# A hybrid encoder trunk: scores in pairs, one product for the meta tokens' values, and output blocks added to the residual in DRAM

## The chip, the core and the metric

The kernel runs on one core of a Trainium2 chip. The metric is the device time of one execution in microseconds (us), lower is better. The engines are named as in the profile: PE (TensorE matmul) with PEld (its weight load), DVE (VectorE), ACT (ScalarE), POOL (GpSimd) and SP (SyncE, which here only issues DMAs). A DMA that adds to its destination (an accumulating DMA) is issued from POOL in this kernel, a plain one from SP.

## What is computed

One inference step of two layers over 656 tokens: 16 meta tokens, 512 prompt tokens and 8 streams of 16 new tokens each. Model width 1024, stored transposed as 8 blocks of 128 channels x 656 tokens. Cut to what matters here:

```python
def trunk_layer(x, p, ...):
    h = rmsnorm(x, p['g_mix'])
    proj = h @ p['w_in']                       # 24 blocks of 128 columns
    # A) attention, 4 heads, two score maps per head: p0 - lam * p1
    oa = diff_attention(qa, k_all, v_all, ...)
    # B) a causal convolution module (ob), C) a gated linear recurrence (oc)
    mix = concatenate([oa, ob, oc])
    x = x + mix @ p['w_out']                   # output projection, residual
    h2 = rmsnorm(x, p['g_ffn'])
    gate, val = split(h2 @ p['w_up'])
    x = x + (gelu(conv3(gate)) * val) @ p['w_down']

def diff_attention(q, k, v, ...):
    s = einsum('bqhcd,bkhcd->bhcqk', q, k) * scale + bias   # c = 0, 1
    p = softmax(where(mask, s, NEG))
    a = p[:, :, 0] - lam * p[:, :, 1]
    return einsum('bhqk,bkhd->bqhd', a, v)
```

## The kernel before

**Products.** A large product runs as three passes with float32r operands (`mm3`, line 398): the weight's high part times the input's high and low parts, and the weight's low part times the input's high part. ACT casts the high part of a weight (`whi`, line 384), DVE subtracts to get the low part (`wlo`, line 385; `ghi`, `glo` where the parts are kept apart). The raw weights come through four buffers (`raw`), so that a weight load can be issued only when the split of an earlier load is done.

**Stages of a layer.** (1) The input projection, 24 column blocks `d_i`, with attention, convolution and recurrence advancing between them as generators. (2) The output projection. Its first six rows of blocks (convolution, recurrence, heads 0 and 1) are the products `d_oa`, for the 8 output blocks m = 0 to 7; the remaining two (heads 2 and 3) are the products `d_ob`, again for m = 0 to 7, with 12 matmuls for each m. (3) The first three column blocks of `w_up` as one group (`e_u`), which take the inputs `hi_h` and `lo_h` made from the finished blocks x(0) to x(7); the norm factor `r_h` of these blocks, which needs all eight; the factors for a Strassen scheme (`factors`, lines 1068 to 1090, on DVE, POOL and ACT); then the feed-forward loop, whose down projections are added into the residual in DRAM.

**The residual.** `xs[m]` is an SBUF tile, `x_scr` (`xdr`) the same eight blocks in DRAM. Before the change every output block m was loaded (`x_in`, line 448, from the kernel's input in layer 0 and from `x_scr` in layer 1) in the `d_oa` loop. `add_x` (line 441, DVE) added the two halves of the `d_oa` product to it from PSUM, and later the two halves of the `d_ob` product; then `x_out` (line 444) wrote the block to `x_scr`, `sq_add` (lines 432, 437) squared and summed it for the norm, and `split` (lines 359, 360) made `hi_h`, `lo_h`.

**Attention.** For each head, queries are in four tiles t = 0 to 3 of 128 rows; tile t sees 144 + 128 t keys. `scores` makes two score maps c = 0, 1 (line 515; the two use different halves of the partitions), which DVE reads from PSUM with bias and maximum (line 517). `turn` transposes the probabilities by 128 keys, counted from key 0, with the last 16 keys left over; `pv` multiplies by the values: tile t takes t + 1 products with 128 keys and one with 16 keys (lines 551, 554, 556), into a PSUM tile `po` of its own.

**What sets the order.** Within a layer's stages (1) to (3) a scheduler orders the instructions of each engine from data dependences, buffers (57 slots of 128 x 656 floats, tag S; 3 + 5 PSUM banks) and the order in which they are written. Each engine then works through its list in that order, SP too: a DMA issue that has to wait holds the issues behind it. Only the feed-forward loop has an order by hand.

Of the kernel before, what the change touches and what calls it, by code (L numbers as in the profile page):

```python
# [13 lines left out]
ALU = mybir.AluOpType  # L14
# [7 lines left out]
T = 656  # L22
# [137 lines left out]
def trunk_kernel(ctx: ExitStack, tc: tile.TileContext, i: dict, o: dict, depth: int = 2):  # L160
# [45 lines left out]
    ident, b64 = sm_("id"), sm_("b64")  # L206
# [235 lines left out]

    def x_out(m):
        nc.sync.dma_start(out=xdr[m], in_=xs[m][:, :T])
# [5 lines left out]
    def tok_major(src, nm):  # L450

        ps = PB(f"tm_{nm}")
        for j in range(4):
            PE.transpose(ps[:, j * 128:(j + 1) * 128], src[:, j * 128:(j + 1) * 128], ident)
        ps2 = PB(f"tm2_{nm}")
        PE.transpose(ps2[:, :128], src[:, 528:656], ident)
        PE.transpose(ps2[:16, 128:256], src[:, 512:528], ident)
        t = S(f"tok_{nm}")
        A.copy(t[:, :512], ps)
        A.copy(t[:, 512:640], ps2[:, :128])  # L460
        t2 = small.tile([16, 128], F32, tag="tok2", name="tok2", bufs=2)
        A.copy(t2, ps2[:16, 128:256])
        return t, t2


    def attention(l, h, got, mix):
# [33 lines left out]
        def scores(t):  # L500
# [7 lines left out]
            ps = PB(f"sc{l}{h}{t}") if t == 0 else None  # L508
            for c in range(2):
                for n in range(nn):  # L510
                    if t > 0:
                        ps, o0 = PB(f"sc{l}{h}{t}{c}{n}"), 0
                    else:
                        o0 = c * 256
                    PE.matmul(ps[:, o0:o0 + w], lhsT=q[64 * c:64 * c + 64, q0:q0 + 128],  # L515
                              rhs=k[64 * c:64 * c + 64, n * w:(n + 1) * w], start=True, stop=True)
                    V.tensor_tensor_reduce(out=p[c][:, n * w:(n + 1) * w], in0=ps[:, o0:o0 + w],
                                           in1=E8[:, TP - nk + n * w:TP - nk + (n + 1) * w], op0=ALU.add, op1=ALU.max,
                                           accum_out=mx[:, n * 2 + c:n * 2 + c + 1], scale=0.125, scalar=-3.0e38)
# [12 lines left out]

        def turn(t):
            nk = 144 + 128 * t
            p = P.pop(t)
            aT = S(f"aT{l}{h}{t}")
            ps = PB(f"aTp{l}{h}{t}")
            for j in range(t + 1):
                PE.transpose(ps[:, j * 128:(j + 1) * 128], p[:, j * 128:(j + 1) * 128], ident)
            ps2 = PB(f"aTq{l}{h}{t}")  # L540
            PE.transpose(ps2[:16, :128], p[:, nk - 16:nk], ident)
            A.copy(aT[:, :(t + 1) * 128], ps[:, :(t + 1) * 128])
            A.copy(aT[:16, 512:640], ps2[:16, :128])
            AT[t] = aT

        def pv(t):
            q0 = 16 + 128 * t
            aT = AT.pop(t)
            po = PB(f"po{l}{h}{t}")
            for j in range(t + 1):  # L550
                PE.matmul(po[:, :128], lhsT=vt[:, j * 128:(j + 1) * 128], rhs=aT[:, j * 128:(j + 1) * 128], start=j == 0,  # L551
                          stop=False)
            if t < 3:
                PE.matmul(po[:, :128], lhsT=vt[:16, (t + 1) * 128:(t + 2) * 128], rhs=aT[:16, 512:640], start=False, stop=True)
            else:
                PE.matmul(po[:, :128], lhsT=vt2, rhs=aT[:16, 512:640], start=False, stop=True)
            A.copy(oh_[:, q0:q0 + 128], po[:, :128])
# [71 lines left out]
        def s_out():  # L629
            a, t = sv["a"], sv["t"]  # L630
            ps = PB(f"sp{l}{h}")
            PE.matmul(ps[:, :128], lhsT=vt[:, 512:640], rhs=a[:, 256:384], start=True, stop=True)
            PE.matmul(ps[:, 128:144], lhsT=vt[:16, 0:128], rhs=a[:16, 384:400], start=True, stop=True)
# [19 lines left out]
        pv(3)  # L653
# [5 lines left out]
        pv(2)  # L659
# [4 lines left out]
        pv(1)  # L664
        s_pv()
        yield
        pv(0)
# [469 lines left out]
    for l in range(depth):  # L1137
# [5 lines left out]
        xsrc = i["x"] if l == 0 else xdr  # L1143
# [24 lines left out]
        with ExitStack() as behind:  # L1168
# [4 lines left out]
            if l == 0:  # L1173
                setup()
        for n in range(3):
            got[order[n]] = evict_r(ps3[n], r, f"e{l}{n}")
# [34 lines left out]
        for m in range(8):  # L1211
            advance(front)
            x_in(m, xsrc)
            ps = gemm(nxt, ka, mix, f"oa{l}{m}", cx)
            add_x(m, ps, cx)
# [10 lines left out]
        for m in range(8):  # L1226
            ps = gemm(nxt, kb, mix, f"ob{l}{m}", cx)
# [81 lines left out]
        def down(n, last=False):  # L1309
# [5 lines left out]
            def step(m):  # L1315
# [8 lines left out]
                def take():  # L1324
                    if not last:

                        d = S(f"dd{l}{n}{m}")
                        for ps, (a, b) in zip(res.pop(m), cy):
                            A.copy(d[:, a:b], ps[:, :b - a])
                        G.dma_start(out=xdr[m][:, a0:T], in_=d[:, a0:T], accum_op=ALU.add)  # L1330
# [159 lines left out]
```

## Time and profile before

| | |
|---|---|
| time, median of 3 runs | 1680.81 us (1680.68 to 1682.55) |
| the profiled execution | 1678.91 us, span of its instructions 1677.1 us |
| PE busy | 1618.5 us, 97% of the span |
| DVE, ACT, POOL busy | 1245.9, 879.1, 566.8 us (74%, 52%, 34%) |
| DMA | 180.56 MB, mean 108 GB/s |
| layer 0: input projection, output projection, from there to the feed-forward loop's steady part | 26 to 310, 310 to 387, 387 to 465 us |
| layer 1: the same | 858 to 1137, 1137 to 1212, 1212 to 1315 us |

Times inside the execution are counted from the span's start. A row of a timeline gives start, duration, engine, line, operation, output and inputs, and in brackets how long the engine had been idle and what ended the wait. A float32 matmul leaves two records, one for each of two passes; a float32r one leaves one. Matmuls are pipelined: one row of `mm3` lasts 0.31 us, but the next starts 0.15 us after it.

### The profile page before, as it was taken

What the parts mean: (1) busy time and instruction counts of PE and PEld (TensorE: products, weight loads), DVE (VectorE), ACT (ScalarE), POOL (GpSimd) and SP (SyncE); (2) the same over time, 40 slices, a digit from 0 to 9 for tenths busy, and PEclk for the clock granted to TensorE, in tenths of its full rate; (3) what the DMA queues carried; (4) which work ended last, traced back from release to release, by engine and by line L of the source; (5) the groups of instructions that cost most, each with busy time, mean ns of one, the idle gap of its engine ahead of it and who ended that gap; (6) DMA issues with size and microseconds to landing.
All of it is one profiled execution on the core that took longest, in us unless ns stands there. A gap on an engine that the chain in (4) does not pass through costs nothing.

```text
span 1677.1 us, 28733 instructions
## 1 busy us (share of the span) xinstructions
PE 1618.5 (97%) x10774; PEld 1527.1 (91%) x10774; DVE 1245.9 (74%) x2391; ACT 879.1 (52%) x1744; POOL 566.8 (34%) x652
## 2 busy tenths in 40 slices
PE   7999999999899999999999999999999999999997
PEld 7898888898899999999998988888988899999997
DVE  6579985769987767666647898856899777777556
ACT  6656576543554444444437556566545444444444
POOL 0102220007556555554001032100276545554420
PEclk9999999999999999999999999999999999999999
DMA  6236441342144444444532364313511344444453
GB/s 226 74 95 160 111 105 36 113 136 99 45 119 102 102 106 106 105 106 112 190 103 81 95 149 98 99 56 130 179 39 51 98 105 102 102 106 99 108 136 122
DMA packets 75003, 180.56 MB, mean 108 GB/s; under 512 B 12752, under 2 KB 18384, under 8 KB 74864
## 3 DMA queue, kind: packets, MB, share of 16 engines
q1 hardware_dynamic: 62192, 149.36, 27.6%
q0 software_dynamic: 12672, 29.37, 11.2%
q8 instruction: 84, 1.38, 0.3%
q14 instruction: 55, 0.45, 0.1%
HBM read 129.80 MB, written 35.46 MB: 99 GB/s over the span
## 4 chain that ended last, share of the span: by engine, by line
PE 78%; DVE 11%; issue 4%; POOL 3%; ACT 2%; DMA 1%; SPq 0%; POOLq 0%; DVEq 0%; ACTq 0%
PE d_dn L398 16%; PE d_i L398 16%; PE d_v L398 12%; PE d_g L398 12%; PE d_oa L398 5%; PE sc L515 2%; PE e_i L398 1%; PE hl L809 1%; PE po L551 1%; DVE fh L1090 1%; DVE wlo L385 1%; PE d_fin L398 1%; PE e_u L398 1%; DVE wlo L992 1%; POOL gv L1299 1%
## 5 line engine op out<-in xcount | busy, mean ns | idle before, releaser
L398 PE MATMUL d_v<-fh,whi 128*128 128x328 f32 (+1 forms) x1120 | 251.8, 312 | 1.6 <-ACT whi L991 1.6
L384 ACT CAST whi<-raw 128x384 fp32r<-128x384 f32 (+2 forms) x243 | 132.6, 548 | 208.8 <-PE d_i L398 76.5
L398 PE MATMUL d_g<-fh,whi 128*128 128x328 f32 (+1 forms) x1008 | 226.5, 312 | 0.3 <-ACT whi L991 0.3
L398 PE MATMUL d_i<-hi_h,whi 128*128 128x328 f32 x672 | 219.3, 326 | 0.0
L398 PE MATMUL d_i<-lo_h,whi 128*128 128x328 f32 x672 | 213.9, 318 | 0.0
L398 PE MATMUL d_i<-hi_h,wlo 128*128 128x328 f32 x672 | 212.9, 317 | 0.0
L398 PE MATMUL d_dn<-hi_g,wlo 128*128 128x328 f32 (+1 forms) x640 | 199.8, 312 | 2.8 <-DVE wlo L385 2.8
L398 PE MATMUL d_dn<-hi_g,whi 128*128 128x328 f32 (+1 forms) x640 | 200.2, 313 | 1.9 <-ACT hi_g L356 1.7
L398 PE MATMUL d_dn<-lo_g,whi 128*128 128x328 f32 (+1 forms) x640 | 200.1, 313 | 1.8 <-DVE lo_g L357 1.8
L385 DVE TENSOR_TENSOR wlo<-raw,whi 128x384 fp32r<-128x384 f32 (+2 forms) x243 | 170.9, 717 | 30.5 <-ACT whi L384 22.7
L398 PEld LDWEIGHTS d_v<-fh,whi 128*128 128x128 f32 x1120 | 189.3, 189 | 2.2 <-ACT whi L991 2.2
L992 DVE TENSOR_TENSOR wlo<-wcb,whi 128x512 fp32r<-128x512 f32 x152 | 131.9, 868 | 74.9 <-ACT whi L991 72.3
L398 PE MATMUL d_v<-fh,wlo 128*128 128x328 f32 (+1 forms) x560 | 175.5, 313 | 3.3 <-DVE wlo L992 3.3
L398 PEld LDWEIGHTS d_g<-fh,whi 128*128 128x128 f32 x1008 | 170.4, 189 | 0.5 <-ACT whi L991 0.5
L398 PE MATMUL d_g<-fh,wlo 128*128 128x328 f32 (+1 forms) x504 | 157.8, 313 | 2.3 <-DVE wlo L992 2.3
L985 POOL TENSOR_TENSOR wcb<-raw 128x512 f32<-128x512 f32 x76 | 109.6, 1442 | 127.8 <-DMA raw<-in_w_up 80.2
L992 DVE TENSOR_TENSOR wlo<-raw,whi 128x512 fp32r<-128x512 f32 x114 | 114.8, 1008 | 50.7 <-ACT whi L991 50.5
L991 ACT CAST whi<-wcb 128x512 fp32r<-128x512 f32 x152 | 93.7, 620 | 110.6 <-PE d_g L398 33.3
L398 PEld LDWEIGHTS d_i<-hi_h,whi 128*128 128x128 f32 x672 | 127.5, 190 | 10.1 <-issue 5.6
L398 PEld LDWEIGHTS d_i<-lo_h,whi 128*128 128x128 f32 x672 | 127.6, 190 | 3.8 <-issue 1.3
L398 PEld LDWEIGHTS d_i<-hi_h,wlo 128*128 128x128 f32 x672 | 127.2, 189 | 3.0 <-issue 1.3
L398 PEld LDWEIGHTS d_dn<-hi_g,wlo 128*128 128x128 f32 x640 | 121.1, 189 | 3.5 <-DVE wlo L385 3.5
(394 smaller groups left out, 4026.9 us busy)
## 6 DMA issues: line engine op xcount, KB each, us to landing
raw<-in_w_up SPq DMA_DIRECT2D x88, 512.0 KB, 3.7
raw<-in_w_in SPq DMA_DIRECT2D x45, 512.0 KB, 3.7
raw<-in_w_down SPq DMA_DIRECT2D x48, 384.0 KB, 3.8
x_scr<-x SPq DMA_DIRECT2D x24, 328.0 KB, 3.2
x_scr<-dd POOLq DMA_DIRECT2D x24, 328.0 KB, 4.5
x<-x_scr SPq DMA_DIRECT2D x24, 328.0 KB, 4.4
x_scr<-dd POOLq DMA_DIRECT2D x24, 320.0 KB, 4.6
cvb<-cvt POOLq DMA_DIRECT2D x20, 328.0 KB, 5.0
```

Of the source, the lines that this page charges most:

```text
L384: seq(A.copy(hi[:, :n], raw[:, a:a + n]))
L385: seq(V.tensor_tensor(out=lo[:, :n], in0=raw[:, a:a + n], in1=hi[:, :n].bitcast(F32), op=ALU.subtract))
L398: PE.matmul(ps[:, :b - a], lhsT=ww[:, n], rhs=r[:, a:b], start=first and j == 0, stop=last and j == 2)
L515: PE.matmul(ps[:, o0:o0 + w], lhsT=q[64 * c:64 * c + 64, q0:q0 + 128], rhs=k[64 * c:64 * c + 64, n * w:(n + 1) * w], start=True, stop=True)
L551: PE.matmul(po[:, :128], lhsT=vt[:, j * 128:(j + 1) * 128], rhs=aT[:, j * 128:(j + 1) * 128], start=j == 0, stop=False)
L809: PE.matmul(ps[:, c * 128:(c + 1) * 128], lhsT=kk[:, 16 + 128 * c:144 + 128 * c], rhs=both(m0 + 64 * c, 64), start=True, stop=True)
L985: G.tensor_tensor(out=t, in0=x, in1=y, op=op)
L991: A.copy(hi, x)
L992: V.tensor_tensor(out=lo, in0=x, in1=hi.bitcast(F32), op=ALU.subtract)
L1090: V.tensor_tensor(out=lo, in0=x, in1=hi.bitcast(F32), op=ALU.subtract)
L1299: G.tensor_tensor(out=v[:, a0:TP], in0=v[:, a0:TP], in1=a[:, a0:TP], op=ALU.mult)
```

## The change

- **Scores.** For each key part the products of c = 0 and c = 1 are issued one after the other, into two PSUM banks, before DVE reads the first of them. For t = 0 both maps shared one bank before.
- **Values.** The blocks of 128 keys now start at key 16 and the 16 meta tokens stand apart. Their probabilities of all four query tiles are kept in one tile `aTm`, and one product of 16 keys x 512 queries (`po`, line 555 of the changed kernel) replaces four of 16 keys x 128. All value products of a head stand in one place, behind its last transposition, in one PSUM bank, and one ACT copy of 512 columns replaces four of 128.
- **First output blocks.** The `d_oa` product goes from PSUM through ACT into a tile `do` (`to_x`), and an accumulating DMA from POOL adds it to `x_scr`. In layer 0 the eight blocks are written to `x_scr` at the start. `x_in(m)` moves from the `d_oa` loop into the `d_ob` loop, where it reads `x_scr`; `add_x`, `x_out`, `sq_add` and `split` of the `d_ob` loop stay.

```diff
+    def to_x(m, ps, cc, nm):
+        d = S(nm)
+        for p, (a, b) in zip(ps, cc):
+            A.copy(d[:, a:b], p[:, :b - a])
+        G.dma_start(out=xdr[m][:, cc[0][0]:T], in_=d[:, cc[0][0]:T], accum_op=ALU.add)
...
-            for c in range(2):
-                for n in range(nn):
-                    if t > 0:
-                        ps, o0 = PB(f"sc{l}{h}{t}{c}{n}"), 0
-                    else:
-                        o0 = c * 256
-                    PE.matmul(ps[:, o0:o0 + w], lhsT=q[64 * c:64 * c + 64, q0:q0 + 128],
+            for n in range(nn):
+                pair = []
+                for c in range(2):
+                    pair.append(PB(f"sc{l}{h}{t}{c}{n}"))
+                    PE.matmul(pair[c][:, :w], lhsT=q[64 * c:64 * c + 64, q0:q0 + 128],
                               rhs=k[64 * c:64 * c + 64, n * w:(n + 1) * w], start=True, stop=True)
-                    V.tensor_tensor_reduce(out=p[c][:, n * w:(n + 1) * w], in0=ps[:, o0:o0 + w],
+                for c in range(2):
+                    V.tensor_tensor_reduce(out=p[c][:, n * w:(n + 1) * w], in0=pair[c][:, :w],
...
+        def pv():
+            po = PB(f"po{l}{h}")
+            PE.matmul(po, lhsT=vt2, rhs=aTm[:16, :512], start=True, stop=False, skip_group_check=True)
+            for t in (3, 2, 1, 0):
+                aT = AT.pop(t)
+                for j in range(t + 1):
+                    PE.matmul(po[:, t * 128:(t + 1) * 128], lhsT=vt[:, j * 128:(j + 1) * 128],
+                              rhs=aT[:, j * 128:(j + 1) * 128], start=False, stop=j == t, skip_group_check=True)
+            A.copy(oh_[:, 16:528], po)
...
             if l == 0:
                 setup()
+                for m in range(8):
+                    x_out(m)
...
         for m in range(8):
             advance(front)
-            x_in(m, xsrc)
             ps = gemm(nxt, ka, mix, f"oa{l}{m}", cx)
-            add_x(m, ps, cx)
+            to_x(m, ps, cx, f"do{l}{m}")
...
         for m in range(8):
+            x_in(m, xdr)
             ps = gemm(nxt, kb, mix, f"ob{l}{m}", cx)
             add_x(m, ps, cx)
             x_out(m)
```

SP's list in layer 0, from the last loads of the `d_oa` loop to the blocks' way out. Before (`x` with its number is the tile of one block):

```order
L448 DMA x_3954<-in_x 128x656
L448 DMA x_4006<-in_x 128x656
L367 DMA raw<-in_w_up 128x1024
L976 DMA gpast_4062<-in_state_ffn 128x352
L367 DMA raw<-in_w_up 128x1024 x2
L367 DMA raw<-in_w_out 128x256 x7
L444 DMA x_scr<-x_3460 128x656
L367 DMA raw<-in_w_up 128x1024
L444 DMA x_scr<-x_3598 128x656
L367 DMA raw<-in_w_up 128x1024
L444 DMA x_scr<-x_3718 128x656
L444 DMA x_scr<-x_3798 128x656
```

And SP's list of the changed kernel at the same place:

```order
L977 DMA gpast_4042<-in_state_ffn 128x352
L367 DMA raw<-in_w_out 128x256 x3
L455 DMA x_4074<-x_scr 128x656
L367 DMA raw<-in_w_out 128x256 x2
L367 DMA raw<-in_w_up 128x1024
L451 DMA x_scr<-x_4074 128x656
L455 DMA x_4105<-x_scr 128x656
L367 DMA raw<-in_w_up 128x1024
L451 DMA x_scr<-x_4105 128x656
L455 DMA x_4137<-x_scr 128x656
L367 DMA raw<-in_w_up 128x1024
L451 DMA x_scr<-x_4137 128x656
```

Before, all eight loads stood ahead of the first write; now the load of block m + 1 stands behind the write of block m, for all eight blocks and in both layers. The first three loads of `w_up` stand ahead of `gpast` in the changed list.

PE's list at the last value product of head 0 in layer 0 (`po` the output, `aT` the transposed probabilities, `tok_v` the values). Before, where the other three tiles' products stand 53 to 192 rows earlier:

```order
L551 MATMUL po_1396<-aT_1275,tok_v_652 128x128
L554 MATMUL po_1396<-aT_1275,tok_v_652 128x128
```

And now:

```order
L555 MATMUL po_1388<-aTm_667,tok_663 128x512
L559 MATMUL po_1388<-aT_866,tok_v_660 128x128 x4
L559 MATMUL po_1388<-aT_985,tok_v_660 128x128 x3
L559 MATMUL po_1388<-aT_1144,tok_v_660 128x128 x2
L559 MATMUL po_1388<-aT_1272,tok_v_660 128x128
```

The ten products with 128 keys moved to one place, and one of 512 columns stands ahead of them in place of four of 128 columns.

## Rows read from the trace of the kernel before

**Rows 1.** The page, parts 1 and 5: busy times; one group of splits.

```profile
PE 1618.5 (97%) x10774; PEld 1527.1 (91%) x10774; DVE 1245.9 (74%) x2391; ACT 879.1 (52%) x1744; POOL 566.8 (34%) x652
...
L385 DVE TENSOR_TENSOR wlo<-raw,whi 128x384 fp32r<-128x384 f32 (+2 forms) x243 | 170.9, 717 | 30.5 <-ACT whi L384 22.7
```

**Rows 2.** Busy time by stretch: length, PE, PEld, DVE, ACT, POOL, clock, DMA.

```profile
257.00:310.00 53.00, 52.23 (x346) 44.89 (x339) 32.56 (x75) 33.47 (x72) 1.69 (x8) 1.00 0.19 60
310.00:369.40 59.40, 58.63 (x416) 54.20 (x417) 36.26 (x92) 30.19 (x74) 2.45 (x5) 1.00 0.38 123
369.40:397.80 28.40, 24.51 (x153) 23.04 (x153) 26.68 (x39) 17.44 (x29) 12.84 (x8) 1.00 0.58 198
397.80:465.00 67.20, 60.31 (x379) 58.00 (x377) 62.10 (x89) 31.46 (x60) 43.91 (x49) 0.97 0.11 33
```

**Rows 3.** Timeline of SP in layer 0's last down projection, where blocks are reloaded.

```profile
821.89 0.40 SPq L448 DMA_DIRECT2D x<-x_scr  x1
...
826.98 0.32 SPq L444 DMA_DIRECT2D x_scr<-x  x1
827.41 0.37 SPq L448 DMA_DIRECT2D x<-x_scr  x1
...
848.66 0.37 SPq L448 DMA_DIRECT2D x<-x_scr  x1
```

**Rows 4.** Timeline of DVE in the same stretch: the additions that wait for these loads.

```profile
830.88 0.91 DVE L441 TENSOR_TENSOR x<-d_dn,x 128x328 f32<-128x328 f32 x2 [0.46 <-DMA x<-x_scr]
...
853.82 0.91 DVE L441 TENSOR_TENSOR x<-d_dn,x 128x328 f32<-128x328 f32 x2 [3.13 <-DMA x<-x_scr]
```

**Rows 5.** Timelines of PE and DVE, layer 0, from `d_ob` to the factors.

```profile
369.24 0.31 PE L398 MATMUL d_ob<-hi_mx,whi 128*128 128x328 f32 x1
...
386.70 0.31 PE L398 MATMUL d_ob<-hi_mx,wlo 128*128 128x328 f32 x1
...
388.49 0.48 DVE L441 TENSOR_TENSOR x<-d_ob,x 128x328 f32<-128x328 f32 x1
...
391.90 0.83 DVE L437 TENSOR_TENSOR sq<-sq,sq 128x656 f32<-128x656 f32 x1
...
396.25 1.48 DVE L319 SCALAR_TENSOR_TENSOR r_h<-rt_h,r_h 128x656 f32<-128x656 f32 x1
397.77 12.38 DVE L1068 SCALAR_TENSOR_TENSOR x<-x,cst,r_h 128x656 f32<-128x656 f32 x8
...
419.60 0.39 PE L398 MATMUL d_g<-hi_h,ghi 128*128 128x328 f32 x1 [0.74 <-DVE gp L1248]
...
422.56 0.64 PE L398 MATMUL d_g<-hi_h,glo 128*128 128x328 f32 x1 [2.41 <-DVE glo L385]
```

**Rows 6.** Timeline of DVE, layer 1: the norm factor's last instruction.

```profile
1221.13 1.23 DVE L319 SCALAR_TENSOR_TENSOR r_h<-rt_h,r_h 128x644 f32<-128x644 f32 x1
```

**Rows 7.** PE at head 0's values, layer 0; a float32 product of 328 columns.

```profile
92.07 1.16 PE L551 MATMUL po<-aT,tok_v 128*128 128x128 f32 x8
93.16 0.48 PE L556 MATMUL po<-aT,tok 16*128 16x128 f32 x2
93.57 0.55 PE L539 MATMUL aTp<-cst,p 128*128 128x128 f32 x3
...
264.36 2.21 PE np_ln L314 x8
```

**Rows 8.** Timeline of PE: one score product of tile 0, and the next.

```profile
107.73 0.51 PE L515 MATMUL sc<-e,e 64*128 64x144 f32 x2
108.17 0.42 PE L611 MATMUL sa<-selw,pown 96*128 96x48 f32 x2
```

**Rows 9.** Short stretches around PE's waits in rows 5, columns as in rows 2.

```profile
420.00:424.00 4.00, 1.59 (x6) 1.45 (x6) 3.86 (x7) 3.78 (x5) 2.56 (x9) 0.80 0.00 0
424.00:428.00 4.00, 4.00 (x23) 4.00 (x22) 3.26 (x6) 3.52 (x7) 3.28 (x2) 0.78 0.41 131
428.00:432.00 4.00, 4.00 (x29) 4.00 (x28) 3.25 (x10) 3.62 (x10) 1.94 (x3) 1.00 0.42 131
```

More of the change, by code (lines that the diff above doesn't have):

```diff
@@ L453, in tok_major @@
         for j in range(4):
-            PE.transpose(ps[:, j * 128:(j + 1) * 128], src[:, j * 128:(j + 1) * 128], ident)
+            PE.transpose(ps[:, j * 128:(j + 1) * 128], src[:, 16 + j * 128:144 + j * 128], ident)
         ps2 = PB(f"tm2_{nm}")
         PE.transpose(ps2[:, :128], src[:, 528:656], ident)
-        PE.transpose(ps2[:16, 128:256], src[:, 512:528], ident)
+        PE.transpose(ps2[:16, 128:256], src[:, 0:16], ident)
         t = S(f"tok_{nm}")
@@ L507, in scores @@
             w = nk // nn
-            ps = PB(f"sc{l}{h}{t}") if t == 0 else None
-            for c in range(2):
-                for n in range(nn):
-                    if t > 0:
-                        ps, o0 = PB(f"sc{l}{h}{t}{c}{n}"), 0
-                    else:
-                        o0 = c * 256
-                    PE.matmul(ps[:, o0:o0 + w], lhsT=q[64 * c:64 * c + 64, q0:q0 + 128],
+            for n in range(nn):
[3 more added lines that the diff above has]
+                    PE.matmul(pair[c][:, :w], lhsT=q[64 * c:64 * c + 64, q0:q0 + 128],
                               rhs=k[64 * c:64 * c + 64, n * w:(n + 1) * w], start=True, stop=True)
-                    V.tensor_tensor_reduce(out=p[c][:, n * w:(n + 1) * w], in0=ps[:, o0:o0 + w],
+                for c in range(2):
+                    V.tensor_tensor_reduce(out=p[c][:, n * w:(n + 1) * w], in0=pair[c][:, :w],
                                            in1=E8[:, TP - nk + n * w:TP - nk + (n + 1) * w], op0=ALU.add, op1=ALU.max,
@@ L531, in scores @@
             P[t] = p[0]
+        aTm = S(f"aTm{l}{h}")
         def turn(t):
-            nk = 144 + 128 * t
             p = P.pop(t)
@@ L538, in turn @@
             for j in range(t + 1):
-                PE.transpose(ps[:, j * 128:(j + 1) * 128], p[:, j * 128:(j + 1) * 128], ident)
+                PE.transpose(ps[:, j * 128:(j + 1) * 128], p[:, 16 + j * 128:144 + j * 128], ident)
             ps2 = PB(f"aTq{l}{h}{t}")
-            PE.transpose(ps2[:16, :128], p[:, nk - 16:nk], ident)
+            PE.transpose(ps2[:16, :128], p[:, 0:16], ident)
             A.copy(aT[:, :(t + 1) * 128], ps[:, :(t + 1) * 128])
-            A.copy(aT[:16, 512:640], ps2[:16, :128])
+            A.copy(aTm[:16, t * 128:(t + 1) * 128], ps2[:16, :128])
             AT[t] = aT
[L546 to L557, printed above, removed]
+        def pv():
[7 more added lines that the diff above has]
+            A.copy(oh_[:, 16:528], po)
         x = qx[h % 2]
@@ L632, in s_out @@
             PE.matmul(ps[:, :128], lhsT=vt[:, 512:640], rhs=a[:, 256:384], start=True, stop=True)
-            PE.matmul(ps[:, 128:144], lhsT=vt[:16, 0:128], rhs=a[:16, 384:400], start=True, stop=True)
+            PE.matmul(ps[:, 128:144], lhsT=vt2, rhs=a[:16, 384:400], start=True, stop=True)
             for g in range(2):
@@ L652, in attention @@
         yield
-        pv(3)
         turn(2)
@@ L658, in attention @@
         turn(1)
-        pv(2)
         s_turn()
@@ L663, in attention @@
         turn(0)
-        pv(1)
         s_pv()
         yield
-        pv(0)
+        pv()
         s_out()
@@ L1142, in trunk_kernel @@
         col = [cols[a] // 128 + b for a, b in order]
-        xsrc = i["x"] if l == 0 else xdr
         got, mix = {}, {}
@@ L1325, in take @@
                     if not last:
[L1327 to L1330, printed above, removed]
+                        to_x(m, res.pop(m), cy, f"dd{l}{n}{m}")
                     else:
```

## The prediction

> **What bounds the kernel now.** I read the page's shares first: PE is busy for 97% of the span [rows 1], so what is taken off another engine is worth nothing unless PE waits for it. Then the busy times by stretch: in the input projection and in the stage of the `d_oa` products PE works 52.23 of 53.0 and 58.63 of 59.4 us, while from `d_ob` to the factors it works 24.51 of 28.4 and DVE 26.68, and in the stretch behind that 60.31 of 67.2 and DVE 62.10 [rows 2]. So there are two kinds of place. In the first two stretches PE is the bound, and a matmul less is time won, one for one. Around `d_ob` DVE is as full as PE, and who waits for whom has to be read from the timelines. There the first `d_ob` matmul starts at 369.24 and the last at 386.70; the last half of block 7 is added at 388.49; the squares are summed at 391.90; the norm factor `r_h` is ready at 397.73 (396.25 + 1.48); the factors follow at once; and PE, done with `e_u` and one further product, twice waits for DVE, 0.74 us for `gp` and 2.41 us for `glo`, both behind the factors on DVE [rows 5]. So in this stage the end is set by DVE's list from `r_h` on, and `r_h` waits for block 7. Call the start of the first `d_ob` matmul S: `r_h` is ready at S + 28.5.
>
> **The change, part by part.**
>
> *Blocks reloaded in the `d_ob` loop.* This is the large term. SP's list now reads, for each block, load, write, next load. SP works through its list in order, so the load of block m + 1 is issued only when the write of block m could be, that is when DVE has finished block m. That finish in turn waits for the load of block m. The eight loads have become a chain of eight, where all were ahead before.
>
> The trace has this very chain. In layer 0's last down projection the blocks are reloaded and written in the same order on SP. There a load follows the write by 0.43 us (826.98 to 827.41) [rows 3]; the addition starts when the load has landed, 3.47 us after the issue (827.41 to 830.88) in one case and 5.16 (848.66 to 853.82) in another, each time with DVE idle until then [rows 3, 4]; and both halves are added in 0.91 us [rows 4]. From 821.89 to 848.66 there are five steps in 26.77 us, 5.35 each [rows 3]. Each step there also holds one 512 KB weight load beside the load and the write of a block, as most of the first steps do here. I take 5.4 us; the bounds are 4.8 (3.47 + 0.91 + 0.43) and 6.5 (5.16 + 0.91 + 0.43).
>
> The chain's start: the load of block 0 stands behind weight loads whose buffers are freed by splits of `w_up` on DVE, and four such splits are now queued behind the low parts of heads 2 and 3 when the `d_oa` products end. At 0.72 us for a split [rows 1] I estimate S + 3.8 for its issue, between S and S + 5.5 (all splits first). With 4.0 us to its landing (5.35 - 0.91 - 0.43) and seven steps of 5.4, the addition of block 7 starts at S + 45.6 and ends 0.9 later, at S + 46.5. Before, 3.8 us passed from its end to the end of the sum of squares (388.97 to 392.73), with splits between them that now lie in the chain's gaps: I take 1.7, the square and the sum at about 0.83 each. From the sum to `r_h` it is 5.0 us (392.73 to 397.73) [rows 5]. So `r_h` is ready at S + 53.2 instead of S + 28.5: 24.7 us later.
>
> Is there cover? PE is ahead by its banks only: three banks hold the `d_ob` products, so PE stops after a block and a half, and the last two thirds of `e_u` need banks that block 7 frees. Those 123 matmuls at 0.15 us, the norm's product (about 1) and one product of 48 matmuls (7.2) then end at about S + 46 + 27 = S + 73. `glo`, for which PE waited at 422.56 (S + 53.3) [rows 5], comes 24.7 later, at S + 78. So DVE still ends last and the whole 24.7 us stand on the path. In layer 1 `r_h` was ready at 1222.36 [rows 6], 27.9 us after its first `d_ob` matmul by the same reading; there I take 25.0. Together **+49.7 us**, bounds +34 (steps of 4.8, first load at S + 1) and +66 (steps of 6.5).
>
> *A page on this price.* The Trainium skill, "DMA: Bandwidth & Descriptors", section "Anatomy of one DMA", fits 2.0 us and bytes / 436e3 (for transfers issued by GpSimd). For a block of 335,872 bytes that is an estimate of 2.8 us where the rows show 3.47 to 5.16; the step would be 4.1 us and the result some 23 us lower than mine. The measured rows decide.
>
> *Output blocks through ACT and POOL.* In the `d_oa` stage 16 additions on DVE for each layer go, 16 copies on ACT and 8 accumulating DMAs on POOL come. DVE worked 36.26, ACT 30.19 and POOL 2.45 of 59.4 us there and PE 58.63 [rows 2]: nothing is won by lighter DVE, and 16 copies of about the same half microsecond bring ACT to some 38, which PE covers. A copy that comes late would hold one of three banks, which gives PE about 2.7 us before it notices (18 matmuls at 0.15). I take 0. The eight writes at the start of layer 0 put 8 x 0.43 = 3.4 us [rows 3] ahead of four weight loads on SP; those weights are needed only after the first three blocks and one more, so I take 0, bounds 0 and 3.4.
>
> *Values.* Four products with 128 keys took 1.09 us (92.07 to 93.16), 0.27 each, and the one with 16 keys 0.41 (93.16 to 93.57) [rows 7]. A head has ten of the first and four of the second: 4.3 us. A product of 512 columns is priced from 328 columns, 2.21 us for 8 passes or 0.276 for a pass [rows 7]: two passes of 512/328 x 0.276 are 0.86 us. A head now costs 2.7 + 0.86 = 3.6, 0.77 us less; eight heads 6.2 us, nearly all where PE is the bound. Putting the products in one place saves further entries into a run of small products; I add 1 us.
>
> *Scores.* For t = 0 a product of 144 columns took 0.44 us (107.73 to 108.17) [rows 8], alone; two side by side on different halves of the partitions may share time. From 0 to 0.44 us for each of 8 heads: I take 1 us. The other tiles had separate banks already. DVE, ACT and POOL keep their work and are covered by PE. Longer lives of the transposed probabilities (four more slots of 57 for each head) may make a tile wait for a slot: bounds 0 and 8 us for all heads. Attention together: **-8 us**, bounds -13 and +2.
>
> **Sum.** 49.7 - 8 = +41.7 on the profiled execution's 1678.91 us: 1720.6. The median of three lies 1.9 above that execution, so the forecast is **1723 us**, 2.5% slower.
>
> **The rivals.**
> - *Not slower: the loads stay ahead.* If an issue that waits did not hold the issues behind it, all loads would have landed before `d_ob`, the chain would vanish and -8 us remain: 1673 us. It decides at a step of about 1.9 us, (28.5 - 0.9 - 1.7 - 5.0 - 7.8) / 7 with the same start. Against it: DVE's idle rows that end with the load, one step after another [rows 4]. 3%.
> - *The clock falls and stays low.* PE will work 1.8 us (12 matmuls) of each 5.4. After PE had waited in 420 to 424 the granted clock was 0.80 there and 0.78 in the next 4 us, and 1.00 after that [rows 9]: between them 3.4 us at the lower of its two levels (1.2 instead of 2.4 GHz), 1.7 us lost. In the `d_ob` loop even doubled matmuls (3.6 us) fit into a step, and 1.7 us in `e_u` fit under the 5 us between S + 73 and S + 78. But if all of `e_u`'s rest ran at the lower level, 18.5 us more less 5 of cover would be added in each layer: +27, 1750 us. 7%. The Trainium skill, "TensorE: Matmul & The Clock Gate", section "HAM oscillation", speaks for it: it says that where PE's work for each block is shorter than the wait for the next block's DMA, PE falls back to the lower clock for every block. The rows here agree that a wait brings the clock down, and show it recovering.
> - *Every load is as slow as the slowest row.* The accumulating DMAs of the last blocks, the writes and 512 KB loads share the queues: 5.16 instead of 4.0 for each is 8 x 1.1 x 2 = +18, 1741 us. 9%.
> - *Slots cost what the products save.* Attention at +2 instead of -8: 1733 us. 7%.
> - *The first load is early and the steps short* (4.8): 1708 us. 9%.
>
> **How the numbers follow.** The forecast has 65%, the rivals 35%. The range for 8 in 10 is **1706 to 1744 us**: below, the shortest step; above, the slowest loads; 1673 and 1750 stay outside. A measurement of this kernel tells apart about 0.2%, 3.4 us. Slower by more than that: all but the first rival and an unnamed rest, **0.95**; within 0.2%: **0.02**; faster: **0.03**.
>
> **What would show it.** In SP's timeline around S: write and load side by side, 0.43 us apart, eight pairs some 5.4 us from each other. On DVE: `x<-d_ob` with idle time that ends with the load of `x`. On PE: waits of `d_ob` and `e_u` for DVE of some 3 us each, 20 to 25 us in each layer, and a lower granted clock there. `r_h` ready about 53 us after the first `d_ob`, and `d_g` still waiting for `glo`. The input projection shorter by about 8 us over both layers. The prediction is wrong if the loads are issued without waiting for the writes, if PE's wait for `glo` vanishes (then `e_u` ends last), or if the input projection is longer than before.

## The result, and the profile after

The changed kernel takes **1729.59 us** (median of 5, 1724.44 to 1733.73) against 1682.18 us for the kernel before, run beside it: a ratio of 1.028, 95% interval 1.0258 to 1.0302. It is 2.8% slower; the forecast was 2.5% and 1723 us, range 1706 to 1744. The profiled execution took 1726.23 us with a span of 1724.5, which is 47.4 us more than the span of before (1677.1).

The first view is part 1 of the page of the changed kernel:

```profile
PE 1632.0 (95%) x10726; PEld 1536.6 (89%) x10726; DVE 1222.5 (71%) x2359; ACT 888.1 (51%) x1752; POOL 582.3 (34%) x668
```

Beside [rows 1], PE has 48 matmul records less and is "busy" 13.5 us longer, yet its share falls: there is new idle time, and some of the work runs at a lower clock. Where the 47.4 us lie is read from the first row of each tile in PE's timelines and the last instruction of `r_h` on DVE:

| stretch (us) | before | after | difference |
|---|---|---|---|
| start to the first `d_i`, layer 0 | 42.4 | 44.4 | +2.0 |
| first `d_i` to first `d_ob`, layer 0 | 326.8 | 325.4 | -1.5 |
| first `d_ob` to `r_h` ready, layer 0 | 28.5 | 54.3 | **+25.8** |
| `r_h` to the first down projection, layer 0 | 63.6 | 61.7 | -1.9 |
| from there to the first `d_i` of layer 1 | 408.7 | 407.6 | -1.0 |
| first `d_i` to first `d_ob`, layer 1 | 324.3 | 325.2 | +0.8 |
| first `d_ob` to `r_h` ready, layer 1 | 28.1 | 52.5 | **+24.4** |
| `r_h` to the first down projection, layer 1 | 90.5 | 88.5 | -2.0 |
| from there to the end | 364.2 | 365.0 | +0.7 |

All of the loss is in the two `d_ob` stages, and the gain that was expected of attention is missing. SP's timeline of the changed kernel in layer 0, where S, the first `d_ob`, is at 369.75:

```profile
374.92 0.44 SPq L455 DMA_DIRECT2D x<-x_scr  x1
...
380.52 0.33 SPq L451 DMA_DIRECT2D x_scr<-x  x1
380.90 0.42 SPq L455 DMA_DIRECT2D x<-x_scr  x1
...
385.81 0.32 SPq L451 DMA_DIRECT2D x_scr<-x  x1
386.23 0.37 SPq L455 DMA_DIRECT2D x<-x_scr  x1
...
412.45 0.32 SPq L451 DMA_DIRECT2D x_scr<-x  x1
412.87 0.37 SPq L455 DMA_DIRECT2D x<-x_scr  x1
```

A load stands 0.37 to 0.43 us behind each write, and from the second load (380.90) to the eighth (412.87) there are six steps, 5.33 us on average (4.58 to 6.65). DVE's timeline in the same stretch:

```profile
384.87 0.91 DVE L441 TENSOR_TENSOR x<-d_ob,x 128x328 f32<-128x328 f32 x2 [1.59 <-DMA x<-x_scr]
387.33 1.60 DVE L360 SCALAR_TENSOR_TENSOR lo_h<-x,cst,hi_h 128x656 fp32r<-128x656 f32 x1 [1.55 <-ACT hi_h L359]
388.85 0.41 DVE L385 TENSOR_TENSOR wlo<-raw,whi 128x256 fp32r<-128x256 f32 x1
389.95 0.91 DVE L441 TENSOR_TENSOR x<-d_ob,x 128x328 f32<-128x328 f32 x2 [0.69 <-DMA x<-x_scr]
...
396.60 0.91 DVE L441 TENSOR_TENSOR x<-d_ob,x 128x328 f32<-128x328 f32 x2 [2.19 <-DMA x<-x_scr]
...
401.25 0.89 DVE L441 TENSOR_TENSOR x<-d_ob,x 128x328 f32<-128x328 f32 x2
...
416.96 0.89 DVE L441 TENSOR_TENSOR x<-d_ob,x 128x328 f32<-128x328 f32 x2
...
423.16 0.84 DVE L319 SCALAR_TENSOR_TENSOR r_h<-rt_h,r_h 128x656 f32<-128x656 f32 x1
```

The additions of five of the eight blocks wait for their loads, as forecast; those of the other three (at 401.25, 405.89 and 416.96) follow DVE's own work without a pause. And most of the 4 us that a load takes is filled by a sequence of DVE's own: 1.55 us of waiting for ACT's `hi_h`, then `lo_h`, then the split of a weight, and only then the next addition. DVE's waits from S to `r_h` (us in total, times, longest), and busy times of that stretch in both kernels (length, PE, PEld, DVE, ACT, POOL, clock, DMA), after first:

```profile
DVE lo_h L360 <- ACT hi_h L359: 10.9, 7, 1.6
DVE x L441 <- DMA x<-x_scr: 6.8, 5, 2.2
DVE wlo L385 <- ACT whi L384: 2.8, 2, 1.7
```

```profile
369.75:424.00 54.25, 35.31 (x158) 32.13 (x157) 30.90 (x45) 21.58 (x37) 15.93 (x11) 0.72 0.56 171
```

```profile
369.24:397.73 28.49, 24.60 (x155) 23.13 (x154) 26.65 (x38) 17.56 (x29) 12.77 (x8) 1.00 0.58 198
```

DVE was busy for 26.65 of 28.49 us before; now it is busy for 30.90 and idle for 23.35. Of the 25.8 us that were added, 4.3 are work and 21.5 idle time, and only 6.8 of the idle time ends with a load. That is the reading which the experiments had to settle. PE's side of it, its waits in that stretch and behind it:

```profile
PE d_ob L398 <- DVE x L441: 18.6, 7, 6.9
...
PE d_g L398 <- DVE glo L385: 1.8, 1, 1.8
```

PE waits 18.6 us for additions and later still 1.8 us for `glo`, where it waited 2.41 before [rows 5]: DVE's list ends last, as before.

### The profile page after: what moved, and what is told of

Same layout as the page of the kernel before. It is cut to its first block, busy times and chain, and to the rows that moved or that the text cites. A ratio compares the mean times of both kernels' runs of the same rounds, so it can differ in the third digit from the quotient of the medians.

```text
span 1724.5 us, 28685 instructions
## 1 busy us (share of the span) xinstructions
PE 1632.0 (95%) x10726; PEld 1536.6 (89%) x10726; DVE 1222.5 (71%) x2359; ACT 888.1 (51%) x1752; POOL 582.3 (34%) x668
## 5 line engine op out<-in xcount | busy, mean ns | idle before, releaser
L385 DVE TENSOR_TENSOR wlo<-raw,whi 128x384 fp32r<-128x384 f32 (+2 forms) x243 | 164.3, 691 | 55.1 <-ACT whi L384 51.4
```

The lines of the kernel that those rows point to most:

```text
L385: seq(V.tensor_tensor(out=lo[:, :n], in0=raw[:, a:a + n], in1=hi[:, :n].bitcast(F32), op=ALU.subtract))
```

## The experiments

All times are medians beside the kernel before on the same chip (1679.75 to 1680.32 us there). The last column is the time from the first `d_ob` to `r_h` in layers 0 and 1; it is 28.5 and 28.1 before and 54.3 and 52.5 in the changed kernel.

| kernel | us | ratio to before, 95% | `d_ob` to `r_h`, us |
|---|---|---|---|
| attn_only | 1680.06 | 0.9991 to 1.0012 | 28.3, 27.9 |
| out_only | 1725.63 | 1.0258 to 1.0289 | 53.5, 53.0 |
| load_1ahead | 1709.70 | 1.0160 to 1.0208 | 45.4, 42.7 |
| loads_ahead | 1703.53 | 1.0129 to 1.0162 | 40.6, 41.2 |
| loads_pool | 1701.14 | 1.0107 to 1.0141 | 37.5, 35.9 |
| writes_pool | 1721.48 | 1.0224 to 1.0266 | 51.0, 49.7 |
| split_lag | 1724.69 | 1.0250 to 1.0286 | 53.4, 51.4 |
| writes_pool_split_lag | 1720.05 | 1.0227 to 1.0258 | 49.6, 49.3 |
| attn_values | 1680.69 | 0.9995 to 1.0012 | 28.2, 28.0 |
| values_in_place | 1673.71 | 0.9946 to 0.9974 | 28.3, 28.1 |
| values_in_place2 | 1673.23 | 0.9945 to 0.9973 | 28.2, 28.1 |
| values_in_place_old_scores | 1676.56 | 0.9970 to 0.9988 | 28.3, 28.0 |

### The two parts alone: attn_only, out_only

attn_only is the changed kernel with the old output blocks (`...` marks what is cut):

```diff
-                for m in range(8):
-                    x_out(m)
...
+            x_in(m, xsrc)
             ps = gemm(nxt, ka, mix, f"oa{l}{m}", cx)
-            to_x(m, ps, cx, f"do{l}{m}")
+            add_x(m, ps, cx)
...
-            x_in(m, xdr)
             ps = gemm(nxt, kb, mix, f"ob{l}{m}", cx)
```

out_only is the kernel before with just these lines as in the changed one.

> The attention part alone (scores in pairs, values in one place with one product for the meta tokens); the output blocks take the old way through add_x, with the loads in the d_oa loop. Theory A (the prediction's price of the products holds, and the output blocks' new way takes part of it back at the start and in the d_oa stage): 8 us less than before, 1674. Theory B (the products save about half of that; the marks in the trace of the changed kernel stand 2.3 us closer from the first d_i to the first d_oa in layer 0 and 1.5 in layer 1): 1678, or 4 us less than before. Theory C (what the products save is lost to later values, longer lives and DVE): within 1.5 us of before.

> The output blocks' part alone (d_oa products through ACT and an accumulating DMA, blocks reloaded in the d_ob loop, eight writes at the start); attention as before. The chain of loads behind writes is in it whole. By the prediction +49.7 us, 1732. Theory A (attention saved 8 in the changed kernel): 1738. Theory B (attention saved 4): 1734. Theory C (attention saved nothing): 1730.

The attention part moves nothing (theory C: 1680.06 against 1680.32), and the output blocks carry the loss: 45 us (1725.63), with the same 53 us from `d_ob` to `r_h`. That is below all three values expected of out_only (1730 to 1738): its two `d_ob` stages are longer by 49.9 us, as priced, but from `r_h` to the first down projection each layer is 2 us shorter. In out_only the stage of the `d_oa` products lasts 59.35 us (59.37 before): the copies on ACT and the accumulating DMAs cost nothing there, as forecast.

### Loads ahead of the writes: loads_ahead, load_1ahead, loads_pool

```diff
             to_x(m, ps, cx, f"do{l}{m}")
+            if m > 1:
+                x_in(m - 2, xdr)
...
+        for m in (6, 7):
+            x_in(m, xdr)
         gpast = ffn_state(l)
...
-            x_in(m, xdr)
             ps = gemm(nxt, kb, mix, f"ob{l}{m}", cx)
```

load_1ahead writes `x_in(0)` ahead of `gpast` and `x_in(m + 1)` in place of `x_in(m)`. loads_pool is loads_ahead with these loads issued from `nc.gpsimd` instead of `nc.sync`.

> The changed kernel with the load of block m written two blocks behind its accumulating DMA in the d_oa loop, so that on SP seven of the eight loads of a layer stand ahead of the first write of a block. Chain theory (each load waits on SP behind the write of the block before): both layers lose the 25 us again, 1680 us, r_h some 29 us behind the first d_ob. Rival (the loads are late because the additions in DRAM land late, or because a load behind an accumulating DMA is slow): the wait moves along with the load, 1715 to 1730 us. Rival (loads that wait on SP now hold the weight loads of the d_oa stage): d_ob starts later than 60 us after the first d_oa, 1690 us or more.

> The changed kernel with each load written one block earlier: on SP load 3 then stands behind write 1, load 5 behind write 3, load 7 behind write 5, and load 1 behind write 0, so that half as many round trips are on the chain. Chain theory: four steps of 5.3 us less in each layer, some 21 less wherever nothing else comes last, so that r_h is some 33 to 38 us behind the first d_ob and the time 1690 to 1700 us. Rival (the price is of the loads themselves and not of their order): within 5 us of the changed kernel, 1725 to 1730 us.

> As loads_ahead, but the loads of the blocks are issued from POOL, two blocks behind the accumulating DMA there, so that SP's list holds no load that waits for an addition in DRAM, and the w_out loads of the d_ob products do not stand behind one. In loads_ahead r_h was still 40.6 us behind the first d_ob (28.5 before), and DVE waited 4.24 us for a weight whose load stood on SP behind the load of block 7. Chain theory with that second cause (SP's order, once for the blocks, once for the weights): r_h about 29 to 33 us behind the first d_ob in both layers and 1680 to 1688 us. Rival (the remaining 12 us are of blocks that land late whatever the queue, or of DVE's extra load): r_h stays near 40 us, 1700 us or more.

The direction is the chain's, the size is not. The changed kernel stood 47.4 us above the kernel before that was run beside it. With loads one block earlier 29.4 us of that are left, so that 18 are won where 30 to 40 were expected; with all loads ahead 23.2 (loads_ahead) and 21.4 (loads_pool) are left, so that 24 to 26 are won, not the 50 of the chain theory. In loads_ahead, SP's list shows a second wait of its own kind:

```profile
368.48 1.46 SPq L455 DMA_DIRECT2D x<-x_scr  x2
...
376.75 0.32 SPq L455 DMA_DIRECT2D x<-x_scr  x1
...
379.56 0.38 SPq L367 DMA_DIRECT2D raw<-in_w_out  x1
```

The eighth load has to wait for its addition in DRAM until 376.75 and holds the weight loads of the later `d_ob` blocks. The first of these goes out at 379.56, ACT casts it at 382.96 after 6.61 us without work, and DVE waits 4.24 us for that, until 383.40. Issued from POOL (loads_pool) the loads hold no weight load, and that stage is 3 to 5 us shorter, but the time is only 2.4 us lower: 1701, where the rival had 1700 or more. What is left there, DVE's waits and busy times in loads_pool from S (371.88) to `r_h`:

```profile
DVE rt_h L317 <- ACT rt_h L316: 2.2, 2, 1.7
DVE wlo L385 <- ACT whi L384: 2.0, 2, 1.1
DVE lo_h L360 <- ACT hi_h L359: 0.9, 1, 0.9
```

```profile
371.88:409.40 37.52, 30.49 (x168) 27.13 (x167) 31.29 (x46) 21.50 (x38) 16.05 (x13) 0.91 0.62 197
```

No wait for a load of a block is left, and the waits for `hi_h` are down from 10.9 to 0.9 us: DVE's list is staggered again, with additions of later blocks ahead of an earlier block's `lo_h`. The stage is still 9.0 us longer than before: 4.6 are DVE's work (31.29 against 26.65) and 4.4 idle time. The work is a move. Six `glo` splits, 4.1 us, stand in this stretch in loads_pool and in the changed kernel (3.9 us there), while in the kernel before DVE did them in the `d_oa` stage:

```profile
L385 DVE TENSOR_TENSOR glo<-raw,ghi 128x512 fp32r<-128x512 f32 x6 | 4.0, 688 | 0.4 <-ACT ghi L384 0.4
```

(groups of DVE by line in the kernel before, 310 to 370 us). These six stand in the `d_ob` stage of both layers in every kernel with the output blocks' edit, out_only too, and in the `d_oa` stage in every kernel without it, so it is that edit that moves them. Which of its lines made the scheduler place them later was not isolated. In layer 1 the stage is 7.8 us longer than before; the two stages make 16.8 of the 21 us that loads_pool still loses.

### Cutting the chain without moving the loads: writes_pool, split_lag, both

```diff
             add_x(m, ps, cx)
-            x_out(m)
+            x_out(m, nc.gpsimd)
```

split_lag leaves the writes on SP and puts `hs.append(split(xs[m - 2], ...))` in the place of block m's, the last two behind the loop; writes_pool_split_lag has both edits.

> The changed kernel with one edit: the write of each block in the d_ob loop is issued from POOL instead of SP. The loads keep their place in the d_ob loop, behind weight loads, but none stands behind a write any more. Chain theory (it is the write on the same queue that holds the next load): the steps of 5.3 us vanish, loads go as the weight buffers allow, r_h 30 to 40 us behind the first d_ob, 1685 to 1705 us. Rival (the loads' late place in the program is what costs, whichever queue the writes take): within 5 us of the changed kernel, 1725 to 1730 us.

> The changed kernel with one edit: in the d_ob loop the split of block m (hi_h on ACT, lo_h on DVE) is written two blocks later, so that DVE's list holds the addition of block m + 1 ahead of lo_h of block m. The writes stay on SP. In writes_pool DVE still went block by block, some 4.7 us each: addition, 1.55 us of waiting for hi_h, lo_h, a split of a weight, next addition. Theory of two chains, one on SP (5.3 us a block), one on DVE's list right under it (4.6 to 4.7): with the SP chain left in place this edit gives nothing, 1726 to 1733 us, DVE's waits for hi_h become waits for the load. Rival (DVE's list alone sets the steps, SP's order follows it): 20 us or more less than the changed kernel, below 1710.

> Both edits: writes of the d_ob loop from POOL, and each split two blocks later. Theory of two chains: with both cut, a load waits only behind a weight load whose buffer a split on DVE frees, for which I estimate some 3.3 us a block instead of 5.3 from the rows of writes_pool; 14 us less in each layer than the changed kernel, 1695 to 1706 us, r_h about 40 us behind the first d_ob. Rival (the loads' late place costs what it costs, whatever is cut): as writes_pool, 1717 us or more.

writes_pool was to decide between the chain and the loads' late place, and it speaks mostly for the place: 1721.48, outside both expectations, is 41.7 us above the kernel before, only some 6 us less than the changed kernel's 47.4 (the intervals overlap slightly), although no load stands behind a write. DVE's waits there, and one of its steps:

```profile
DVE lo_h L360 <- ACT hi_h L359: 10.9, 7, 1.6
...
DVE x L441 <- DMA x<-x_scr: 1.9, 3, 1.4
```

```profile
390.93 0.91 DVE L441 TENSOR_TENSOR x<-d_ob,x 128x328 f32<-128x328 f32 x2 [0.18 <-DMA x<-x_scr]
393.38 1.75 DVE L360 SCALAR_TENSOR_TENSOR lo_h<-x,cst,hi_h 128x656 fp32r<-128x656 f32 x1 [1.55 <-ACT hi_h L359]
395.06 0.68 DVE L385 TENSOR_TENSOR wlo<-raw,whi 128x512 fp32r<-128x512 f32 x1
395.66 0.89 DVE L441 TENSOR_TENSOR x<-d_ob,x 128x328 f32<-128x328 f32 x2
```

The waits for loads fall from 6.8 to 1.9 us and those for `hi_h` stay at 10.9. So there are two chains of nearly the same period. One runs over SP (write, load, addition; 5.33 us on average in the changed kernel). The other runs over DVE and ACT (two additions 0.91, then 1.55 until ACT has squared the block and made `hi_h`, `lo_h` 1.6 to 1.8, a split 0.41 to 0.68; the steps in this run are mostly 4.7 us and 4.9 on average). Cutting the first uncovers the second, which already set three of the seven steps of the changed kernel (4.65, 4.64 and 5.45 us). In the kernel before DVE's list was staggered: the additions of later blocks stood ahead of an earlier block's `lo_h`, as this piece of its timeline shows:

```profile
374.29 0.49 DVE L441 TENSOR_TENSOR x<-d_ob,x 128x328 f32<-128x328 f32 x1
374.70 1.63 DVE L385 TENSOR_TENSOR wlo<-raw,whi 128x256 fp32r<-128x256 f32 x1
376.25 0.89 DVE L360 SCALAR_TENSOR_TENSOR lo_h<-x,cst,hi_h 128x656 fp32r<-128x656 f32 x1
377.06 1.30 DVE L441 TENSOR_TENSOR x<-d_ob,x 128x328 f32<-128x328 f32 x3
```

split_lag was meant to cut the second chain and writes_pool_split_lag both. split_lag alone gives 1724.69, just under the 1726 to 1733 expected of two chains and far from its rival's 1710; it is 44.6 us above the kernel before, and with the overlap of the intervals it can't be told from the changed kernel. Both together give 1720.05 where 1695 to 1706 were expected: that expectation fell. The trace shows why the edit did not cut what it should. ACT's timeline in writes_pool_split_lag:

```profile
392.33 0.75 ACT L432 ACTIVATE sq<-x 128x656 f32<-128x656 f32 x1 [2.90 <-DVE x L441]
392.99 0.83 ACT L359 ACTIVATE hi_h<-x,cst 128x656 fp32r<-128x656 f32 x1
393.72 0.61 ACT L384 CAST whi<-raw 128x512 fp32r<-128x512 f32 x1
```

`hi_h` is now of a block two earlier and could have been made long before, but in ACT's list it stands behind `sq` of the block just added, and DVE's next rows wait for it: `lo_h` again starts 1.55 us after the addition. The second chain merely hands over through `sq`. Only the first two steps of this run, where no `lo_h` stands in between yet, are shorter (additions at 379.02, 382.38 and 386.71: 3.36 and 4.33 us; then 4.7, and 5.8 in the last two). What the stage would take with both chains cut, and the loads still late, was not reached: that the second chain sets the steps is read from the rows and not shown by a run without it.

### Where the saving of attention went: attn_values, values_in_place and its mends

attn_values has the new values and the old scores. values_in_place has both attention edits, but `pv(t)` at the places it had before:

```diff
+        def pv(t):
+            if t == 3:
+                pb["po"] = PB(f"po{l}{h}")
...
+            if t == 0:
+                PE.matmul(po, lhsT=vt2, rhs=aTm[:16, :512], start=False, stop=True, ...)
+                A.copy(oh_[:, 16:528], po)
...
+        pv(3)
         turn(2)
         s_scores()
...
         turn(1)
+        pv(2)
         s_turn()
```

In values_in_place the first product of every query tile carries a start flag, which changes what the shared bank sums; values_in_place2 has the flag on the bank's first product alone.

> The kernel before with the new values alone (one product for the meta tokens, all products of a head in one place); scores and output blocks as before. The prediction's price: 7 us less than before, 1673. Theory W (the matmuls are saved, 8.9 us of po in the trace with both attention edits, but at places where PE then waits for DVE and ACT): within 2 us of before, 1679 to 1682.

> Both attention edits, without the output blocks' edit, but the products with 128 keys of each query tile go back to the places that they had before, into one bank that is kept through the head, and the one product for the meta tokens closes it. The saving of matmuls is the same. Theory P (it is the gathering of the values behind the last transposition that costs what they save): 4 to 8 us less than before, 1672 to 1676. Theory W (PE runs up against DVE and ACT wherever it is given less to do): within 2 us of before, or slower by a held bank, 1679 to 1684.

> As values_in_place (which had a start flag on each query tile's first product in the shared bank; here only the first product of the bank has it); the instructions and their places are the same. Output blocks as before. Theory P (it is the gathering that took back what the products save): 1672 to 1676 us, 0.4% less than before. Theory W: 1679 us or more.

> As values_in_place2, with the scores as before (both maps of tile 0 in one bank, DVE's reading of the first map between the two products of a key part). It prices the scores in pairs. By the prediction the pairs save 1 us, so this is 1 us above values_in_place2. Theory N (the pairs are worth nothing that can be measured, as attn_only against attn_values said): within 1.5 us of it.

Theory P holds: the same matmuls, at their old places, give 0.41% (0.27 to 0.55), 6.9 us less than before; gathered in one place they give nothing (1680.06 in attn_only, 1680.69 in attn_values). values_in_place2 is faster than the kernel before and the changed one. PE's time in the value products over both layers' projections (sums for the tile `po`: before, attn_only, values_in_place2) says the opposite at first sight:

```profile
sum 1153.00, PE 37.30 PEld 30.15 ACT 8.33; mean PE 37.30 PEld 30.15 ACT 8.33
```

```profile
sum 1157.00, PE 28.39 PEld 20.80 ACT 4.69; mean PE 28.39 PEld 20.80 ACT 4.69
```

```profile
sum 1157.00, PE 34.33 PEld 23.29 ACT 4.65; mean PE 34.33 PEld 23.29 ACT 4.65
```

Gathered, the products take 8.9 us less; in place, only 3.0 less. But the sums over the four stretches from the first `d_i` to the first `d_ob` of both layers (length, then busy times; same order) show what it is exchanged for:

```profile
sum 651.16, PE 640.33 PEld 565.36 DVE 494.83 ACT 389.66 POOL 91.14; mean PE 160.08 PEld 141.34 DVE 123.71 ACT 97.42 POOL 22.79
```

```profile
sum 655.51, PE 635.70 PEld 555.78 DVE 491.55 ACT 387.58 POOL 94.63; mean PE 158.93 PEld 138.94 DVE 122.89 ACT 96.90 POOL 23.66
```

```profile
sum 646.87, PE 634.64 PEld 556.82 DVE 492.77 ACT 387.77 POOL 93.04; mean PE 158.66 PEld 139.21 DVE 123.19 ACT 96.94 POOL 23.26
```

PE's idle time is 10.8 us before, 19.8 gathered and 12.2 in place. One of the new waits, in attn_only: PE's rows and DVE's around it.

```profile
334.60 0.41 PE L398 MATMUL d_oa<-hi_mx,whi 128*128 128x328 f32 x1 [1.23 <-DVE x L441]
...
338.49 1.12 PE L555 MATMUL po<-aTm,tok 16*128 16x512 f32 x2
339.54 2.50 PE L559 MATMUL po<-aT,tok_v 128*128 128x128 f32 x20
```

```profile
333.78 0.17 DVE L531 RECIPROCAL sm<-sm 128x2 f32<-128x2 f32 x1 [1.97 <-ACT sA L620]
333.98 0.16 DVE L532 TENSOR_TENSOR sm<-sm,neglam 128x1 f32<-128x1 f32 x1
334.05 0.90 DVE L441 TENSOR_TENSOR x<-d_oa,x 128x328 f32<-128x328 f32 x2
```

DVE is held at 333.78 by ACT in the middle of a softmax; the addition that frees PE's banks stands behind that in DVE's list, and PE, which has run ahead through its three banks, waits 1.23 us. The value products that could have filled the gap stand at 338.49. In values_in_place2 two of them (four records) are there just then, and no such wait follows:

```profile
332.67 0.61 PE L560 MATMUL po<-aT,tok_v 128*128 128x128 f32 x4
```

That filling is the cause of the whole difference is argued from the idle times and from such places; it was not traced for each of them. A wait for a slot of the transposed probabilities shows nowhere: in attn_only only the copy of `po` waits for a value product. Another part can lie in the clock: in layer 1's projection of attn_only it falls after a stretch with waits (same columns as [rows 2]).

```profile
1068.56:1077.56 9.00, 7.94 (x34) 4.35 (x32) 8.97 (x16) 6.02 (x11) 4.88 (x5) 0.94 0.34 102
1077.56:1086.56 9.00, 9.00 (x66) 6.44 (x66) 4.55 (x20) 2.46 (x7) 0.50 (x1) 0.68 0.09 33
```

That is worth 9 x 0.06 + 9 x 0.32 = 3.4 us; the kernel before and values_in_place2 each have such a stretch too, in layer 0 (0.81 in 168 to 177, 1.7 us). Averaged over all executions the granted clock is 0.991 in attn_only and 0.992 in values_in_place2, by my estimate some 1.4 of the 6.8 us between them. The scores in pairs are worth 3.3 us by the last two runs (1673.23 against 1676.56, intervals that overlap slightly), more than the 1 us of the prediction and the 1.5 of theory N, and 0.6 by attn_only against attn_values. The mean clock (0.992 against 0.9905) would make 2.5 of the 3.3 us by the same estimate, so they are worth something between nothing and 3 us.

## Why the prediction was right, and which steps were not

**What bounds.** PE in the projections, DVE from `d_ob` to the factors: confirmed, PE still waits for `glo` at the end of the stage.

**The chain on SP.** Its form and period are as forecast: load 0.37 to 0.43 us behind the write, steps of 5.33 us on average (5.4), first load at S + 5.2 (3.8 taken, up to 5.5 allowed), `r_h` at S + 54.25 (53.2) and 52.5 in layer 1, together +50.2 us where +49.7 stood. The load's landing, issue to addition where DVE waited for it, is 3.72 to 5.29 us (386.23 to 389.95, 391.31 to 396.60); for one block for which DVE did not wait it is 3.3 at most (397.96 to 401.25). The Trainium skill, "DMA: Bandwidth & Descriptors", section "Anatomy of one DMA", has a fit for transfers issued by GpSimd, which gives 2.8 us as an estimate for this size; these loads, issued from SP, took longer. With the page's step of 4.1 and its landing of 2.8 the chain would have been 20.6 us too low; the prediction's "some 23 us" is more than its own terms give.

**What it hid.** The prediction put the whole 49.7 us on that chain and said in its first rival that, with all loads landed before `d_ob`, "the chain would vanish and -8 us remain: 1673 us". This counterfactual is the step that failed: with the loads ahead the kernel takes 1701 to 1704, 21 to 23 us above before (that attention's 8 us are missing too is another matter, below). The prediction saw that there are "splits between them that now lie in the chain's gaps", and for the sum it was used in that came true (1.73 us from the last addition to the end of the sum of squares, 1.7 taken). It did not see that DVE's own work nearly fills these gaps. When the loads come late, DVE's and ACT's lists change from staggered to block by block, which alone makes 4.9 us a block (writes_pool), and six splits move into the stage. That the total came out right is in part luck: the longer of two chains of nearly the same period sets the time, and the forecast had the one that is longer in most steps.

**Output blocks through ACT and POOL.** 0 forecast, 0 measured for the `d_oa` stage (59.35 against 59.37 us in out_only); that the edit moves six splits into the `d_ob` stage was not forecast. **The eight writes at the start.** 0 taken; the first `d_i` came 2.0 us later, but it stands at 43.6 to 44.3 us in attn_only, attn_values and values_in_place2, which have no such writes, and at 42.5 and 42.8 in split_lag and writes_pool, which have them. No price can be read.

**Attention.** -8 forecast, within 2 us of 0 measured: the mis-sized term. The price of the products was about right (7.2 us by the sum, 8.9 in the `po` records). The sign that the prediction named, an input projection shorter by about 8 us, shows 3.7 (from the first `d_i` to the first `d_oa`, both layers), and the `d_oa` stages take 3.1 of that back. The step that failed is "Putting the products in one place saves further entries into a run of small products; I add 1 us", together with "DVE, ACT and POOL keep their work and are covered by PE". The gathering costs 6.8 us (1680.06 against 1673.23). The likely reason is that PE's share of 98% left few waits before because these small products stood where DVE and ACT were behind.

**The rivals.** Not slower: out, since the loads did wait for the writes, and even without such waits (loads_pool) 21 us are lost. Clock: PE's granted clock is 0.72 from S to `r_h`, and 1.00 in each 4 us from 424 to 444, so that the rest of `e_u` ran at the upper level. No wait of DVE from S to `r_h` ends with a product of PE, so the low clock lay under DVE's chain and no loss from it shows. The Trainium skill, "TensorE: Matmul & The Clock Gate", section "HAM oscillation", says that PE falls back for every block. The trace agrees in part: the granted clock is 0.50 in 378 to 386 and in 398 to 406, through more than one block, but 1.00 in 390 to 394 in the middle of the loop, and 1.00 behind it. Slots: the saving of attention is missing, as this rival had it, but not through its mechanism (no wait for a slot). Every load as slow as the slowest, short steps: the mean step of 5.33 lies between.

**Not foreseen.** From `r_h` to the first down projection both layers are 2 us shorter, in out_only too; in layer 0 the eight products of the blocks with `r_h` take 10.4 us on DVE where they took 12.4. The forecast was 41.7 us against 47.4: attention and the start make +9.3 of that, the chain +0.5, this -3.9.

## What to carry to other kernels

When a load is moved behind the work it feeds, look at the lists of every engine of that loop, not at the DMA queue alone: a second chain of nearly the same period may lie under the first, and cutting one is then worth only the difference. Small products on a "97% busy" engine can also be its filler; when they are merged, try them where they stood, and count idle time in the stretch, not only the saved matmuls. To price an edit against "as before", run it with the suspected cause taken away; a right total does not show a right cause.

## What the hardware showed that was not expected

In the `d_ob` stage of layer 0 of the changed kernel `lo_h` on DVE takes 0.90 us when POOL is still, and 1.60 to 1.67 in the five blocks where POOL's sum of squares runs beside it. POOL's rows in the changed kernel, against DVE's `lo_h` at 387.33 (1.60 us) above:

```profile
386.65 1.58 POOL L437 TENSOR_TENSOR sq<-sq,sq 128x656 f32<-128x656 f32 x1 [12.74 <-ACT sq L432]
```

The `lo_h` before it, at 382.05, took 0.90 us, and POOL stood idle then. This belongs to the period of the second chain. And with a start flag on the first product of each slice the shared bank of values_in_place does not hold the sum of its products, while one flag on the bank's first product is enough for all four slices.
